# A fourth weight sum and the gate row's multiply-adds, moved behind the last addition to c

## The chip, the cores and the metric

The kernel runs on one core of one Trainium2 chip. Its time is device microseconds from start to end of one execution. The core has TensorE (PE in the profile), VectorE (DVE), ScalarE (ACT), GpSimd (POOL) and SyncE (SP), which here issues the transfers.

## What is computed

One layer: a modulated norm, attention of two kinds, an output projection with a gated residual, and then a gated feed-forward part. The change lies in the last, with 1024 tokens, 1024 channels and 2816 hidden channels:

```python
mod = jnp.dot(jax.nn.silu(c), w_ada[l]) + b_ada[l]
sh_a, sc_a, g_a, sh_m, sc_m, g_m = jnp.split(mod, N_MOD, axis=-1)
...
h = modulate(rmsnorm(x, g_mlp_norm[l]), sh_m, sc_m)
u = causal_dwconv(jnp.dot(h, w_up[l]), conv_w[l], conv_b[l])
gate, val = jnp.split(u, 2, axis=-1)
x = x + g_m[:, None, :] * jnp.dot(jax.nn.silu(gate) * val, w_down[l])
```

All of it is float32. The convolution is causal and has width 3. The vector g_m is the "gate row" of the change's name; it is needed only at the very end.

## The kernel before

The up projection runs over 22 tiles j of 128 gate channels and the 128 value channels that belong to them. Each tile is a 2 by 2 block product in the Strassen-Winograd form: seven products in place of eight, with sums of the weight blocks ahead of them and sums of the products behind them. So that full precision comes out of TensorE's fast float32 form, each operand is split into a high and a low half (`split`), and a product is three matmuls for each of four contraction blocks (`product`, L1067 to L1069), so 84 matmuls a tile.

`ff_tile(j, cur)` does the products of tile j, and between them prepares the weights of tile j+1:

- `ff_load` (L1072) loads two raw weight tiles and splits wa and wb. The high half is a copy on ScalarE (L77), the low half a subtraction on GpSimd (L84).
- `ff_sums` (L1081) makes the sums of the raw blocks on VectorE: L1084 gives wc, L1086 and L1087 give we and wd, and L1091 gives the fourth, wg, from a12 and the block that L1087 left. Each is split as above.
- VectorE adds the products up in `c`, a tile of four blocks: L1277, L1278, L1280 and last L1291, each with one operand in a PSUM bank. ScalarE copies two of the products (L1272 and L1287).
- `conv` (L1217), once for the gate channels and once for the value channels: ScalarE scales c into u (L1220), and VectorE adds the two shifted terms (L1221, L1222). Then come SiLU on ScalarE (L1295) and the product of the two halves on VectorE (L1296).
- The sums that the down projection will need are made on GpSimd: L1303 in even tiles, L1308, L1309 and L1311 in odd ones. They and the products go to DRAM through SyncE's queue (L1262).

`gate_row` is a generator. After two tiles each step loads two pieces of w_ada for the next step (L1196), and does two multiply-adds on VectorE over the two pieces loaded before (L1206 the first time, then L1208, into `gmbc`). Eight such steps are followed by an empty one, and by one that adds the bias (L448), sums over the partitions with TensorE (L449) and copies the row back (L1215). The main loop advances it by one step behind each tile from j = 2 on.

The order on each engine isn't that of the source: a scheduler places the instructions by their dependencies and by its own estimates of time, and the source can only add an order with `tc.issue_after(ins)`, which puts the block's instructions behind `ins` on `ins`'s engine alone. Before the change the scheduler put both L1091 and the gate row's multiply-adds ahead of L1291.

Of the kernel before, what the change touches and what calls it, by code (L numbers as in the profile page):

```python
# [22 lines left out]
MUL, ADD, SUB, MIN, MAX = ALU.mult, ALU.add, ALU.subtract, ALU.min, ALU.max  # L23
# [7 lines left out]
NF = FF // P  # L31
# [33 lines left out]
def layer_kernel(ctx, tc, I, out):  # L65
    nc = tc.nc
    pe, act, dve, pool, sp = nc.tensor, nc.scalar, nc.vector, nc.gpsimd, nc.sync
# [7 lines left out]
    def hi_of(eng, o, i):  # L75
        if eng == "a":
            act.activation(o, i, AF.Copy)  # L77
        elif eng == "p":
            pool.tensor_scalar(o, i, 1.0, 0.0, op0=MUL, op1=ADD)
        else:  # L80
            dve.tensor_copy(o, i)

    def lo_of(eng, o, i, hi):
        (pool if eng == "p" else dve).tensor_tensor(o, i, f32(hi), op=SUB)  # L84
# [30 lines left out]
    def rsqrt_mean(r, ss, n, cols=None):  # L115
        sc = ss if cols is None else ss[:, cols]
        pool.tensor_scalar(sc, sc, 1.0 / n, EPS, op0=MUL, op1=ADD)
        pool.tensor_tensor(r, ss, nhalf[:].to_broadcast(list(r.shape)), op=ALU.pow)
# [31 lines left out]
    def gemm3(pt, pairs, start=True, stop=True):  # L150

        n = len(pairs)
        for i, (sh, sl, mh, ml) in enumerate(pairs):
            pe.matmul(pt, sh, mh, start=(start and i == 0), stop=False)  # L154
            pe.matmul(pt, sh, ml, start=False, stop=False)  # L155
            last = pe.matmul(pt, sl, mh, start=False, stop=(stop and i == n - 1))  # L156
        anchor["pe"] = last.ins
# [119 lines left out]
    for d in range(ND):  # L277
# [22 lines left out]
        for t in range(NT):  # L300
            h, j = divmod(t, 4)
# [705 lines left out]
    def o_load(t):  # L1007
        ol[t] = go.tile([P, 4, P], F32R, name=f"ol{t}", tag="ol", bufs=4)
        oh[t] = go.tile([P, 4, P], F32R, name=f"oh{t}", tag="oh", bufs=4)
        anchor["ol"] = sp.dma_start(f32(ol[t][:]), oT_d[0:4, :, t * P:(t + 1) * P].rearrange("k p t -> p k t")).ins  # L1010
        hi_of("a", oh[t][:], f32(ol[t][:]))
        lo_of("p", ol[t][:], f32(ol[t][:]), oh[t][:])
# [29 lines left out]
    def bpage(nm, k, v, le):  # L1042
        pg = hpools[(nm, k)] if (nm, k) in hpools else h2p.tile([P, 2, 512], F32R, name=f"{nm}_{k}")
        hi_of("a", pg[:, 0], v[:])
        lo_of(le, pg[:, 1], v[:], pg[:, 0])
        B[nm, k] = pg
# [5 lines left out]
    def mt(tag, shape, name, dt=F32):  # L1052
        return mp["a" if tag in ("raw", "w2", "ws") else "b"].tile(list(shape), dt, name=name, tag=tag, bufs=MB[tag])
# [3 lines left out]
    def split(src, nm, tag="ws"):  # L1057
        w = mt(tag, [P, 2, 512], nm, F32R)
        hi_of("a", w[:, 0], src)
        lo_of("p", w[:, 1], src, w[:, 0])  # L1060
        return w
# [10 lines left out]
    def ff_load(j):  # L1072

        raw = []
        for i in range(2):
            r = mt("raw", [P, D], f"wu{i}_{j}")
            sp.dma_start(r[:], I["w_up"][i * NF + j].rearrange("p k m -> p (k m)"))
            raw.append(r)
        return raw, split(raw[0][:, :512], f"wa{j}", "w2"), split(raw[0][:, 512:], f"wb{j}", "w2")

    def ff_sums(j, raw):  # L1081
        a11, a12, a21, a22 = raw[0][:, :512], raw[0][:, 512:], raw[1][:, :512], raw[1][:, 512:]
        t3 = mt("s", [P, 512], f"ws3_{j}") if j else tb.tile([P, 512], F32, name="ws3_0", tag="v", bufs=12)
        dve.tensor_tensor(t3[:], a11, a21, op=SUB)  # L1084
        w = [split(t3[:], f"wc{j}")]
        dve.tensor_tensor(a21, a21, a22, op=ADD)  # L1086
        dve.tensor_tensor(a11, a21, a11, op=SUB)  # L1087
        w.append(split(a11, f"wd_{j}"))
        w.append(split(a21, f"we{j}"))
        w.append(split(a22, f"wf{j}"))  # L1090
        dve.tensor_tensor(a12, a12, a11, op=SUB)  # L1091
        w.append(split(a12, f"wg{j}"))
        return w

    op_ = {t: gb.tile([P, D], F32, name=f"pa{t}", tag="pa", bufs=4) for t in range(4)}

    def x_load(t):
        if t > 3:
            op_[t] = gb.tile([P, D], F32, name=f"pa{t}", tag="pa", bufs=4)
        sp.dma_start(op_[t][:], part_d[t])  # L1100
        ox[t] = tb.tile([P, D], F32, name=f"x1_{t}", tag="x1", bufs=8)
        sp.dma_start(ox[t][:], I["x"][t * P:(t + 1) * P, :])
# [4 lines left out]
    raw0, wa0, wb0 = ff_load(0)  # L1107
# [3 lines left out]
    w0 = None  # L1111
    for t in range(NT):
        pt = ps2.tile([P, 1024], F32, name=f"op{t}", tag="op", bufs=3)
        for n in range(2):
            gemm3(pt[:, n * 512:(n + 1) * 512],
                  [(oh[t][:, k], ol[t][:, k], wo[n][k][:, 0], wo[n][k][:, 1]) for k in range(4)])
        if t + 4 < NT:
            o_load(t + 4)
        pa, x1 = op_[t], ox[t]
        dve.tensor_tensor(pa[:], pa[:], pt[:], op=ADD)  # L1120
        dve.tensor_tensor(pa[:], pa[:], gabc[:], op=MUL)
        dve.tensor_tensor(x1[:], x1[:], pa[:], op=ADD)
        sp.dma_start(x1_d[t], x1[:])
        act.activation(pa[:], x1[:], AF.Square, accum_out=ss2[:, t:t + 1])
        if t + 4 < NT:
            x_load(t + 4)
        rsqrt_mean(r2[:, t:t + 1], ss2[:, t:t + 1], D)
        xn2[t] = x1
        dve.tensor_scalar(x1[:], x1[:], r2[:, t:t + 1], 1.0, op0=MUL, op1=MUL)
        if t == 1:  # L1130
            w0 = ff_sums(0, raw0)
        if t == 4:
            for k in range(ND):
                v0[k] = mod_T(k, 0)
                bpage("b11" if k < 4 else "b21", k % 4, v0[k], "v" if k % 2 else "p")
# [13 lines left out]
    p34 = ps2.tile([P, 1024], F32, name="p34_0", tag="op", bufs=3)  # L1149
# [37 lines left out]
    def bank(tag, name, n=1):  # L1187
        return ps3.tile([P, n * 512], F32, name=name, tag=tag, bufs=2 if tag == "p1" else 1)
# [75 lines left out]
    def ff_tile(j, cur):  # L1264
        wc, wd, we, wf, wg, wb, p1, c = cur
        p34 = bank("p34", f"p34_{j}", 2)
        p5, p6, p7 = bank("p5", f"p5_{j}"), bank("p6", f"p6_{j}"), bank("p7", f"p7_{j}")
        nxt = None
        if j:
            with tc.issue_after(p3_last[0]):  # L1270
                product(p1[:], wb, "b21", add=True)
            act.activation(c[:, 0], p1[:], AF.Copy)  # L1272
            if j == NF - 1:
                early()
            product(p7[:], wc, "t3")
            product(p6[:], wd, "t2")
            dve.tensor_tensor(c[:, 1], c[:, 3], p6[:], op=ADD)  # L1277
            dve.tensor_tensor(c[:, 2], c[:, 1], p7[:], op=ADD)  # L1278
            product(p5[:], we, "t1")
            dve.tensor_tensor(c[:, 1::2], c[:, 1:3], p5[:].unsqueeze(1).to_broadcast([P, 2, 512]), op=ADD)  # L1280
            product(p34[:, 512:], wf, "t4")
        if j + 1 < NF:
            raw, wa, wb = ff_load(j + 1)
            q1 = bank("p1", f"p1_{j + 1}")
            product(q1[:], wa, "b11")
            d = mt("c", [P, 4, 512], f"c{j + 1}")
            act.activation(d[:, 3], q1[:], AF.Copy)  # L1287
            nxt = ff_sums(j + 1, raw) + [wb, q1, d]
        if j:
            p3_last[0] = product(p34[:, :512], wg, "b22")  # L1290
            dve.tensor_tensor(c[:, 1:3], c[:, 1:3], p34[:].rearrange("p (a b) -> p a b", a=2), op=ADD)  # L1291
        cg = c[:, 0:2].rearrange("p a b -> p (a b)")
        cv = c[:, 2:4].rearrange("p a b -> p (a b)")
        ug, uv = conv(cg, j), conv(cv, NF + j)
        act.activation(ug[:], ug[:], AF.Silu)  # L1295
        dve.tensor_tensor(ug[:], ug[:], uv[:], op=MUL)  # L1296
        i = j // 2
        lo, hi = ug[:, :512], ug[:, 512:]
        sm = mt("s", [P, 512], f"gs{j}")
        if j % 2 == 0:  # L1300
            us.append(ug)
            keep(0, 1, i, lo)
            pool.tensor_tensor(sm[:], lo, hi, op=SUB)  # L1303
            keep(6, 1, i, sm[:])
        else:
            ue = us.pop()
            keep(1, 2, i, ug[:])
            pool.tensor_tensor(ue[:, 512:], ue[:, 512:], hi, op=ADD)  # L1308
            pool.tensor_tensor(ue[:, :512], ue[:, 512:], ue[:, :512], op=SUB)  # L1309
            keep(3, 2, i, ue[:])  # L1310
            pool.tensor_tensor(sm[:], lo, ue[:, :512], op=SUB)  # L1311
            keep(5, 1, i, sm[:])
        return nxt

    gr_gen = gate_row()
    p3_last = [last]
    cur = w0 + [None, None, c0]
    for j in range(NF):
        cur = ff_tile(j, cur)
        if j >= 2:  # L1320
            next(gr_gen, None)

    psC.__exit__(None, None, None)
    mlp.__exit__(None, None, None)
# [232 lines left out]
```

## Time and profile before

| what | value |
|---|---|
| runs shown | 1391.5, 1392.78, 1389.2 us (median 1391.5) |
| profiled execution | 1391.56 us, of which the span of instructions is 1389.8 us |
| TensorE, matmuls | 1233.6 us busy, 89% of the span |
| TensorE, weight loads | 1004.4 us, 72% |
| VectorE | 1112.7 us, 80% |
| ScalarE | 617.9 us, 44% |
| GpSimd | 694.8 us, 50% |
| up projection, tiles 2 to 21 | about 785 to 1180 us of the span |
| granted TensorE clock in that stretch | 1.00 |

Busy times are averages over stages of quite different kinds. For the up projection the order in time is read, tile by tile. A row of the timeline has the start in us, the duration in us, the engine, the line, the operation, the output and inputs by name, their shapes, how many such instructions are merged in the row, and in brackets the idle time of the engine ahead of it with what ended it. A row of the waits has the waiting instruction, what it waited for, the sum in us, how many times, and the longest. A row that begins with a line and ends with "x22" and three numbers has the shortest, middle and longest duration in ns.

### The profile page before, as it was taken

How to read it: one execution, taken by the hardware profiler on the slowest of the kernel's cores; microseconds unless marked ns; L12 is line 12 of the kernel's file. 1: busy time of each engine (PE TensorE's matmuls, PEld its weight loads, DVE VectorE, ACT ScalarE, POOL GpSimd, SP SyncE). 2: the span in 40 equal slices, each digit the busy share in tenths (PEclk: the TensorE clock that was granted, in tenths of full speed). 3: DMA queues.
4: the chain of work that ended last, by engine and by line, in shares of the span. 5: the costliest groups of instructions: out<-in, count | busy, mean ns of one | idle time of the engine just before them, and what ended most of it. 6: DMA issues, size and time to landing. Idle time of an engine off the chain costs nothing.

```text
span 1389.8 us, 18690 instructions
## 1 busy us (share of the span) xinstructions
PE 1233.6 (89%) x6156; PEld 1004.4 (72%) x6156; DVE 1112.7 (80%) x1870; ACT 617.9 (44%) x1129; POOL 694.8 (50%) x676
## 2 busy tenths in 40 slices
PE   4889798999777789886887999999999999999998
PEld 3888486987555577665665887777778777888886
DVE  6957888675689987794789798898888888688667
ACT  4343445443555544453365434434443444443331
POOL 5454557375546664353643666657867784200000
PEclk9899798999887889997999999999999999999999
DMA  8413658666313477678821233333223224984441
GB/s 314 131 37 85 142 143 188 155 146 138 74 41 78 87 158 164 127 146 237 302 100 53 91 129 99 121 129 114 99 99 107 84 99 139 322 326 129 129 159 61
DMA packets 223689, 190.57 MB, mean 137 GB/s; under 512 B 148708, under 2 KB 166884, under 8 KB 223592
## 3 DMA queue, kind: packets, MB, share of 16 engines
q1 hardware_dynamic: 223592, 189.38, 48.0%
q8 instruction: 48, 0.79, 0.2%
q14 instruction: 49, 0.40, 0.1%
HBM read 117.24 MB, written 37.49 MB: 111 GB/s over the span
## 4 chain that ended last, share of the span: by engine, by line
PE 40%; DVE 29%; issue 9%; DMA 7%; ACT 7%; POOL 6%; SPq 1%; DVEq 0%; POOLq 0%; ACTq 0%
DVE u L1222 4%; DVE u L1221 4%; PE dnA_P L1368 2%; PE dnA_P L1370 2%; PE dnA_P L1369 2%; PE p L1069 2%; PE p L1067 2%; PE p L1068 2%; PE sm L764 2%; PE sc L758 2%; PE dnB_P L1370 1%; PE dnB_P L1369 1%; PE dnB_P L1368 1%; ACT u L1220 1%; PE pvm L852 1%
## 5 line engine op out<-in xcount | busy, mean ns | idle before, releaser
L77 ACT ACTIVATE dnP<-dnr 128x1024 fp32r<-128x1024 f32 x73 | 77.3, 1061 | 110.9 <-PE dnA_P L1370 46.4
L1342 DVE TENSOR_TENSOR dnP<-dnr,dnP 128x1024 fp32r<-128x1024 f32 x72 | 88.2, 1229 | 46.9 <-ACT dnP L77 46.9
L1221 DVE SCALAR_TENSOR_TENSOR u<-c,cvp,u 128x1023 f32<-128x1023 f32 x44 | 81.7, 1897 | 43.9 <-ACT u L1220 43.9
L73 POOL TENSOR_SCALAR hlm<-Pm,rim 128x512 f16<-128x512 f32 (+3 forms) x96 | 68.4, 722 | 74.0 <-ACT Pm L790 21.0
L1222 DVE SCALAR_TENSOR_TENSOR u<-c,cvp,u 128x1022 f32<-128x1022 f32 x44 | 85.4, 1980 | 0.0
L73 POOL TENSOR_SCALAR hlc<-Pc,ric 128x640 f16<-128x640 f32 (+2 forms) x64 | 46.7, 733 | 69.0 <-DVE ric L793 45.2
L812 DVE SCALAR_TENSOR_TENSOR hlm<-Pm,rim,hlm 128x512 f16<-128x512 f32 (+3 forms) x96 | 67.5, 712 | 8.6 <-POOL hlm L73 8.2
L790 ACT ACTIVATE Pm<-sm,mm 128x128 f32<-128x128 f32 (+3 forms) x64 | 47.2, 738 | 52.1 <-DVE mm L783 26.7
L852 PE MATMUL pvm<-PTm,vt 128*128 128x256 f16 (+1 forms) x320 | 47.4, 301 | 20.9 <-DMA PTm<-hlm 16.8
L790 ACT ACTIVATE Pc<-sc,mc 128x640 f32<-128x640 f32 (+2 forms) x64 | 42.1, 659 | 49.7 <-DVE mc L779 36.5
L812 DVE SCALAR_TENSOR_TENSOR hlc<-Pc,ric,hlc 128x640 f16<-128x640 f32 (+2 forms) x64 | 53.6, 842 | 10.4 <-POOL hlc L73 10.2
L1220 ACT ACTIVATE u<-c,cvp 128x1024 f32<-128x1024 f32 x44 | 52.2, 1234 | 14.9 <-DVE c L1291 7.9
L852 PEld LDWEIGHTS <-vt 128*128 128x128 f16 x320 | 32.5, 111 | 36.2 <-issue 14.8
L77 ACT ACTIVATE wc<-ws 128x512 fp32r<-128x512 f32 x22 | 13.9, 633 | 98.4 <-DVE ws L1084 98.4
L154 PE MATMUL ipq<-wq_s,hT 128*128 128x256 f32 x192 | 55.5, 292 | 0.9 <-ACT wq_s L77 0.9
L155 PE MATMUL ipq<-wq_s,hT 128*128 128x256 f32 x192 | 55.8, 291 | 0.4 <-POOL wq_s L84 0.3
L156 PE MATMUL ipq<-wq_s,hT 128*128 128x256 f32 x192 | 55.3, 289 | 0.0
L1295 ACT ACTIVATE u<-u 128x1024 f32<-128x1024 f32 x22 | 23.4, 1062 | 67.8 <-DVE u L1222 67.8
L1369 PE MATMUL dnA_P<-dnP 128*128 128x512 f32 x132 | 51.3, 389 | 0.0
L1370 PE MATMUL dnA_P<-dnP 128*128 128x512 f32 x132 | 51.3, 389 | 0.0
L1368 PE MATMUL dnA_P<-dnP 128*128 128x512 f32 x132 | 51.2, 389 | 0.0
L84 POOL TENSOR_TENSOR wc<-ws,wc 128x512 fp32r<-128x512 f32 x22 | 35.4, 1611 | 30.5 <-ACT wc L77 30.5
(421 smaller groups left out, 4546.0 us busy)
## 6 DMA issues: line engine op xcount, KB each, us to landing
wu<-w_up SPq DMA_DIRECT2D x44, 512.0 KB, 3.5
dnr<-g_d SPq DMA_DIRECT2D x73, 256.0 KB, 3.6
aw<-w_ada SPq DMA_DIRECT2D x48, 256.0 KB, 3.8
g_d<-u SPq DMA_DIRECT2D x22, 512.0 KB, 2.8
dnr<-w_down SPq DMA_DIRECT2D x44, 256.0 KB, 5.4
adaw<-w_ada_a SPq DMA_DIRECT2D x16, 512.0 KB, 5.9
x<-x SPq DMA_DIRECT2D x16, 512.0 KB, 8.8
g_d<-gs SPq DMA_DIRECT2D x22, 256.0 KB, 2.2
```

Of the source, the lines that this page charges most:

```text
L73: pool.tensor_scalar(o, i, s, 1.0, op0=MUL, op1=MUL)
L77: act.activation(o, i, AF.Copy)
L790: act.activation(pr[:, :n], sv, AF.Exp, bias=m[:], scale=-1.0, accum_out=rsum[:, 0:1])
L812: dve.scalar_tensor_tensor(hl[:, w:2 * w], pp, ri[:], hl[:, :w], op0=MUL, op1=SUB)
L852: last = pe.matmul(dst, u.vst(j), mov, start=(x == 0), stop=(x == len(todo) - 1), skip_group_check=True)
L1220: act.activation(u[:], c, AF.Identity, scale=cvp[:, cv + 2:cv + 3], bias=cvp[:, cv + 3:cv + 4])
L1221: dve.scalar_tensor_tensor(u[:, 1:], c[:, :S - 1], cvp[:, cv + 1:cv + 2], u[:, 1:], op0=MUL, op1=ADD)
L1222: dve.scalar_tensor_tensor(u[:, 2:], c[:, :S - 2], cvp[:, cv:cv + 1], u[:, 2:], op0=MUL, op1=ADD)
L1342: r = f(*a, **k)
L1368: pe.matmul(pt, sh, w[:, 0, 0], start=start, stop=False, skip_group_check=add)
L1369: pe.matmul(pt, sh, w[:, 1, 0], start=False, stop=False, skip_group_check=add)
L1370: pe.matmul(pt, sl, w[:, 0, 0], start=False, stop=stop, skip_group_check=add)
```

## The change

`ff_sums` no longer makes the fourth sum itself, but returns a function that does. `ff_tile` calls it after L1291 has been issued, in a block that puts VectorE's instructions behind L1291. The step of the gate row, which stood behind the tile in the main loop, moves into the same block. Both stand ahead of `conv` in the source now. Tile 0, whose products are made before the loop, has no L1291; its call is not ordered.

```diff
         w.append(split(a22, f"wf{j}"))
-        dve.tensor_tensor(a12, a12, a11, op=SUB)
-        w.append(split(a12, f"wg{j}"))
-        return w
+
+        def rest():
+            dve.tensor_tensor(a12, a12, a11, op=SUB)
+            return split(a12, f"wg{j}")
+        return w, rest
...
-            w0 = ff_sums(0, raw0)
+            w0, rest = ff_sums(0, raw0)
+            w0.append(rest())
...
-            nxt = ff_sums(j + 1, raw) + [wb, q1, d]
+            nxt, rest = ff_sums(j + 1, raw)
         if j:
             p3_last[0] = product(p34[:, :512], wg, "b22")
-            dve.tensor_tensor(c[:, 1:3], c[:, 1:3], p34[:].rearrange("p (a b) -> p a b", a=2), op=ADD)
+            full = dve.tensor_tensor(c[:, 1:3], c[:, 1:3], p34[:].rearrange("p (a b) -> p a b", a=2), op=ADD).ins
+            with tc.issue_after(full):
+                if j + 1 < NF:
+                    nxt.append(rest())
+                if j >= 2:
+                    next(gr_gen, None)
+        else:
+            nxt.append(rest())
+        if j + 1 < NF:
+            nxt += [wb, q1, d]
         cg = c[:, 0:2].rearrange("p a b -> p (a b)")
         cv = c[:, 2:4].rearrange("p a b -> p (a b)")
         ug, uv = conv(cg, j), conv(cv, NF + j)
...
         cur = ff_tile(j, cur)
-        if j >= 2:
-            next(gr_gen, None)
```

Lines of the kernel before are used throughout: L1091 becomes L1093 in the changed kernel, L1291 becomes L1294, L1208 becomes L1211, L1220 to L1222 become L1223 to L1225, L1277 becomes L1280, L1287 becomes L1290 and L1296 becomes L1308.

## The prediction

> **What bounds the kernel now.** I read the page's chain that ended last, then the waits of the up projection (785 to 1180 us), then that stretch in order of time, engine by engine.
>
> ```profile
> PE 40%; DVE 29%; issue 9%; DMA 7%; ACT 7%; POOL 6%; SPq 1%; DVEq 0%; POOLq 0%; ACTq 0%
> ```
>
> ```profile
> DVE u L1221 <- ACT u L1220: 42.2, 20, 2.7
> DVE c L1291 <- PE p L1069: 2.7, 3, 1.7
> ```
>
> VectorE has one hole in a tile: 20 times, 2.1 us each, L1221 waits for ScalarE's L1220. The change puts VectorE work into just this hole. What the hole is used for today decides, and that stands in the order of time of tiles 5 and 6 (start, duration, engine, line):
>
> ```profile
> 851.21 1.40 DVE L1208 SCALAR_TENSOR_TENSOR gmbc<-adaw,cs,gmbc 128x512 f32<-128x512 f32 x2
> 852.53 0.68 DVE L1087 TENSOR_TENSOR wu<-wu,wu 128x512 f32<-128x512 f32 x1
> 853.32 0.69 DVE L1091 TENSOR_TENSOR wu<-wu 128x512 f32<-128x512 f32 x1
> 853.92 1.21 DVE L1291 TENSOR_TENSOR c<-c,p 128x1024 f32<-128x1024 f32 x1
> 857.67 3.52 DVE L1221 SCALAR_TENSOR_TENSOR u<-c,cvp,u 128x1023 f32<-128x1023 f32 x2 [2.53 <-ACT u L1220]
> 861.11 4.54 DVE L1222 SCALAR_TENSOR_TENSOR u<-c,cvp,u 128x1022 f32<-128x1022 f32 x2
> 865.75 1.23 DVE L1296 TENSOR_TENSOR u<-u,u 128x1024 f32<-128x1024 f32 x1
> 866.90 0.68 DVE L1277 TENSOR_TENSOR c<-c,p 128x512 f32<-128x512 f32 x1
> ...
> 870.37 1.67 DVE L1086 TENSOR_TENSOR wu<-wu 128x512 f32<-128x512 f32 x1
> ...
> 874.65 3.41 DVE L1208 SCALAR_TENSOR_TENSOR gmbc<-adaw,cs,gmbc 128x512 f32<-128x512 f32 x2
> 877.99 1.21 DVE L1291 TENSOR_TENSOR c<-c,p 128x1024 f32<-128x1024 f32 x1
> 880.57 4.55 DVE L1221 SCALAR_TENSOR_TENSOR u<-c,cvp,u 128x1023 f32<-128x1023 f32 x2 [1.37 <-ACT u L1220]
> 885.04 2.46 DVE L1222 SCALAR_TENSOR_TENSOR u<-c,cvp,u 128x1022 f32<-128x1022 f32 x2
> 887.61 1.22 DVE L1296 TENSOR_TENSOR u<-u,u 128x1024 f32<-128x1024 f32 x1
> ```
>
> ```profile
> 854.01 1.28 POOL L84 TENSOR_TENSOR wd<-wu,wd 128x512 fp32r<-128x512 f32 x1 [3.28 <-ACT wd L77]
> 855.24 1.30 POOL L84 TENSOR_TENSOR we<-wu,we 128x512 fp32r<-128x512 f32 x1
> 856.49 1.32 POOL L84 TENSOR_TENSOR wf<-wu,wf 128x512 fp32r<-128x512 f32 x1
> 857.74 2.36 POOL L84 TENSOR_TENSOR wa<-wu,wa 128x512 fp32r<-128x512 f32 x1
> 860.07 2.27 POOL L84 TENSOR_TENSOR wg<-wu,wg 128x512 fp32r<-128x512 f32 x1
> 862.30 2.27 POOL L84 TENSOR_TENSOR wb<-wu,wb 128x512 fp32r<-128x512 f32 x1
> 867.12 1.29 POOL L1308 TENSOR_TENSOR u<-u,u 128x512 f32<-128x512 f32 x1 [2.56 <-DVE u L1296]
> ```
>
> The same two L1222 take 2.46 us at 885 us, with GpSimd idle, and 4.54 us at 861 us, with GpSimd subtracting; GpSimd's subtractions take 2.3 us there instead of 1.3. The two engines take turns: one subtraction and one multiply-add come out every 2.24 us or so (857.74, 860.07, 862.30), 1.12 us each. L1208 at 874.65 pays the same price: 3.41 us for the two instead of 1.40, so 1.70 a turn, 1.12 of it GpSimd's and 0.58 its own. L1291 does not collide, since it reads a PSUM bank:
>
> ```profile
> L1291 DVE TENSOR_TENSOR c<-c,p x21: 1206/1214/1222, 774.9 to 1175.3; 128x1024 f32<-128x1024 f32 x21
> ```
>
> So the hole isn't empty. While VectorE does L1291 and then waits, GpSimd runs wd, we and wf 1.24 us apart, at full speed. What is queued is not VectorE but VectorE and GpSimd together. The fourth weight sum, on the other hand, has the cheapest place there is now: GpSimd is waiting for ScalarE's wd, which needs L1087, and so L1091 runs alone (minimum, median and maximum in ns):
>
> ```profile
> L1091 DVE TENSOR_TENSOR wu<-wu x22: 691/692/1758, 667.5 to 1156.8; 128x512 f32<-128x512 f32 x22
> ```
>
> **The Trainium skill** gives the reason on its page "SBUF — State Buffer", section "Who interferes with whom": a Vector instruction with two SBUF inputs contends with a GpSimd instruction that reads SBUF, and the one that starts first holds the pair for its whole instruction. The trace agrees that they exclude each other, but has 2.24 us for a turn of both where the durations alone, 1.28 and 1.20, would add to 2.48. An estimate by that rule, with whole durations as holds, stands at the end of the next part.
>
> **The change part by part.** The built program's order shows that it does what it says: on VectorE L1091 and the gate row's two multiply-adds stand right behind L1291, ahead of both L1221; on ScalarE the high half of wg moves behind both L1220; GpSimd's order is unchanged. Two things come along: in seven gate tiles L1277 moves ahead of L1296, and in some of them TensorE's twelve matmuls of wb come ahead of the last two of wc.
>
> *The fourth sum, a tile without gate row.* I walk from the end of L1087 (853.21) to the end of L1296 (866.98): 13.77 us now. GpSimd's wd begins 0.80 later, L1221 at 4.46 with wd, we and wf behind it. From there turns of 1.12: L1221 to 5.58, wa 6.70, L1221 7.82, wg 8.94, L1222 10.06, wb 11.18, L1222 12.30, then L1296, 1.33 with its gap: 13.63, 0.14 short of the trace. Afterwards: L1291 from 0 to 1.13, wd holds until 1.97, L1091 until 2.53 (a 0.56 turn), we 3.65. Now wf has been asked for before L1220 is done: ScalarE drops wg from its queue ahead of L1220,
>
> ```profile
> 855.88 0.62 ACT L77 ACTIVATE wg<-wu 128x512 fp32r<-128x512 f32 x1
> 856.40 2.37 ACT L1220 ACTIVATE u<-c,cvp 128x1024 f32<-128x1024 f32 x2
> ```
>
> which brings the first L1220 0.52 us forward (856.40 to 855.88), so L1221 is ready at 3.94, but wf has the turn until 4.77. L1221 then ends at 5.89, and six turns and L1296 later it is 13.94. That is 0.17 over the trace, 0.31 over the walk of before; I take 0.24. The 0.7 us that L1091 frees ahead of L1291 is used by nobody, since GpSimd waits for wd through it. In every second tile TensorE's product for L1291 is about due anyway, and L1291 cannot use it fully either; the walk does not change, as wd sets the next turn. Ten such tiles, 2.4 us; with everything absorbed 0, with the 0.7 us lost as well as 0.3, some 7.
>
> *The gate row.* Both walks start at the end of L1086 and take in L1277. Odd tile: now 866.98 - 851.21 + 0.61 = 16.4. After: L1087 0.72, L1291 1.85, wd 2.62, L1091 3.18, we 4.30, L1208 4.88, wf 6.00, L1208 6.58, wa 7.70, four multiply-adds and wg, wb in turns to 14.4, L1277 15.1, L1296 16.4. Nothing gained: the multiply-adds that ran alone at 851.21 now each wait for a subtraction. Even tile, from 872.04 to 888.83 and 0.61: 17.4 now, 17.35 after. There they collide already (3.41 us), so moving them is even.
>
> *L1277 ahead of L1296.* GpSimd waits for L1296 (its 2.56 us at 867.12) and then works through L1277, L1278 and L1280, all PSUM reads, without collision. With L1277 in front, 0.6 us of that cover is gone and L1084 meets a subtraction: walked, 0.3 us in one tile of a pair and 0.4 in the other. Four pairs: 2.6 us; bounds 0 and 5.
>
> *One more gate tile that costs.* The first gate pair now lies in a tile that TensorE bounds:
>
> ```profile
> 793.89 1.22 DVE L1291 TENSOR_TENSOR c<-c,p 128x1024 f32<-128x1024 f32 x1 [1.66 <-PE p L1069]
> ...
> 809.88 0.87 DVE L1206 TENSOR_SCALAR gmbc<-adaw,cs 128x512 f32<-128x512 f32 x2
> ...
> 812.93 1.22 DVE L1291 TENSOR_TENSOR c<-c,p 128x1024 f32<-128x1024 f32 x1 [0.78 <-PE p L1069]
> ...
> 1175.31 1.22 DVE L1291 TENSOR_TENSOR c<-c,p 128x1024 f32<-128x1024 f32 x1
> ```
>
> L1291 still waits 0.78 us behind L1206, so it is free. Behind the L1291 at 812.93 it delays a convolution that nothing covers: 1.4 us (two ops at the 851.21 row's price), bounds 0 and 3.4 (the 874.65 row).
>
> *The rest at nothing.* The closing ops of the gate row
>
> ```profile
> L448 DVE TENSOR_TENSOR gmbc<-gmbc,brow 1x512 f32<-1x512 f32 x2 | 2.3, 1140 | 0.0
> ```
>
> move behind L1291 too and pay there what they pay now, give or take 1 us. The gate row's loads stand one tile earlier in SyncE's queue, still behind the store of u; their buffers, seven to four a tile, were freed a tile before. wg's low half, and with it the load that reuses its raw buffer, ends up to 1.2 us later; its readers come a tile later.
>
> Sum: 2.4 + 2.6 + 1.4 = 6.4 us. The profiled execution took 1391.56 us, the median is 1391.5: 1398.0 us.
>
> By the skill's whole-instruction lock the fourth sum would cost 0.80 + 1.28 + 0.69 + 1.28 + 1.28 - 4.46 = 0.87 a tile, an estimate, and the time would be about 1404 us; no row shows holds that long.
>
> **The rivals.** *The hole is filled for nothing (faster).* If VectorE were what bounds, 18 tiles would save 0.69 each (12.4), and eight gate tiles 1.32 where the hole is 2.53 and 0.68 where it is 1.37 (8.0). TensorE stops that: 793.89 to 812.93, 19.04 us, is a tile in which L1291 waits for it, and 18 of these are 342.7 of the 362.4 us from 812.93 to 1175.31, so at most 19.7 us, about 1372. For it speaks the wait list; against it that GpSimd uses the hole. It decides if a subtraction beside L1091 or L1208 costs under half a turn. Chance 0.12, most of it partial, 1380 to 1387.
>
> *An even exchange.* The turns are the same in number, only their order changes; then 1391.6, and the trace's rows for L1091 grow by what the hole shrinks. Chance 0.22.
>
> *TensorE loses as well (slower still).* With wb ahead of wc's end TensorE stalls on ScalarE's L1287 with more left to do; if L1291 then waits for it in every second tile, some 0.7 us in nine tiles, 6 us more: 1404. Chance 0.10; my forecast has 0.56.
>
> **How the numbers follow.** A measurement of this kernel tells some 0.3%, 4.2 us, from no change: below 1387.3 is faster, above 1395.7 slower. Slower holds the forecast and the last rival, 0.66; same 0.22; faster 0.12. The range, 1389 to 1404, leaves out the faster case and the upper bounds taken together.
>
> **What would show it.** Right: the wait of L1221 for L1220 falls from 42.2 us to well under half, L1091's median rises from 692 ns to 1.2 us or more, L1208's lone 0.74 us ones vanish, wd, we and wf lose their 1.3 us, and L1291 starts in non-gate tiles lie over 39.5 us apart by twos. Wrong: L1091 stays near 0.7 us behind L1291, or the L1291 starts close to 19.04 us.

## The result and the profile after

The changed kernel took 1402.8 us in the middle of its first six runs, against 1390.35 us for the kernel before: ratio 1.0081 (95% interval 1.0052 to 1.0109), slower. Twelve more runs on another occasion, beside new runs of the kernel before, gave 1.0050 (1.0034 to 1.0066), some 7 us. The forecast was 1398.0 us, 6.4 us up.

The profiled execution of the changed kernel took 1406.06 us with a span of 1404.3 us. Most of what follows measures one stretch, from the first start of the last addition to c (L1291 before, L1294 changed) to its last, 20 tiles on. Its ends stand at the right of the row of that line, in us:

```profile
L1294 DVE TENSOR_TENSOR c<-c,p x21: 1207/1214/1222, 781.1 to 1189.8; 128x1024 f32<-128x1024 f32 x21
```

408.7 us. In the kernel before the timeline has the first of these starts at 774.85 and the last at 1175.31 (both rounded in its row in the prediction): 400.5 us. So the stretch lost 8.3 us (408.72 against 400.46). Behind it the two profiles agree: 214.5 us from the last of these additions to the end in both. Ahead of it the changed kernel's profile is 6.2 us later; that part is taken up under the last experiment.

VectorE's waits in the up projection (785 to 1195 us) show that the hole was filled:

```profile
DVE u L1224 <- ACT u L1223: 11.4, 10, 1.4
DVE c L1294 <- PE p L1069: 8.7, 7, 4.1
```

The wait ahead of the convolution fell from 42.2 us to 11.4, yet the stretch became longer. Where the time went is in the durations of the moved instructions (shortest, middle and longest in ns):

```profile
L1093 DVE TENSOR_TENSOR wu<-wu x22: 682/1572/1597, 671.3 to 1172.0; 128x512 f32<-128x512 f32 x22
```

```profile
L1211 DVE SCALAR_TENSOR_TENSOR gmbc<-adaw,cs,gmbc x14: 1775/1784/1790, 842.0 to 973.7; 128x512 f32<-128x512 f32 x14
```

The fourth sum went from 692 ns to 1572, and no multiply-add of the gate row runs alone any more: their middle went from 744 ns to 1784. In the order of time, tile 5 (the first L1294 here is the one at 853.92 us before), VectorE and then GpSimd:

```profile
858.03 1.59 DVE L1086 TENSOR_TENSOR wu<-wu 128x512 f32<-128x512 f32 x1
859.73 0.69 DVE L1087 TENSOR_TENSOR wu<-wu,wu 128x512 f32<-128x512 f32 x1
860.34 1.21 DVE L1294 TENSOR_TENSOR c<-c,p 128x1024 f32<-128x1024 f32 x1
861.47 1.57 DVE L1093 TENSOR_TENSOR wu<-wu 128x512 f32<-128x512 f32 x1
862.96 3.50 DVE L1211 SCALAR_TENSOR_TENSOR gmbc<-adaw,cs,gmbc 128x512 f32<-128x512 f32 x2
866.38 4.54 DVE L1224 SCALAR_TENSOR_TENSOR u<-c,cvp,u 128x1023 f32<-128x1023 f32 x2
870.85 3.50 DVE L1225 SCALAR_TENSOR_TENSOR u<-c,cvp,u 128x1022 f32<-128x1022 f32 x2
874.28 0.67 DVE L1280 TENSOR_TENSOR c<-c,p 128x512 f32<-128x512 f32 x1
874.87 1.21 DVE L1308 TENSOR_TENSOR u<-u,u 128x1024 f32<-128x1024 f32 x1
```

```profile
861.22 1.27 POOL L84 TENSOR_TENSOR wd<-wu,wd 128x512 fp32r<-128x512 f32 x1 [2.15 <-ACT wd L77]
862.45 1.74 POOL L84 TENSOR_TENSOR we<-wu,we 128x512 fp32r<-128x512 f32 x1
864.16 1.75 POOL L84 TENSOR_TENSOR wf<-wu,wf 128x512 fp32r<-128x512 f32 x1
865.87 1.74 POOL L84 TENSOR_TENSOR wa<-wu,wa 128x512 fp32r<-128x512 f32 x1
```

VectorE has no hole at all from 859.73 us to the end of L1308 at 876.08. The subtractions we, wf and wa, which started 1.25 us apart while VectorE waited (we and wf took 1.3 us each), now start 1.71 us apart, each one taking turns with the sum or a multiply-add. Nothing starts earlier: the first L1224 starts 6.8 us behind the end of L1086 (866.38 less 859.62), and before the change the first L1221 started 6.5 us behind it (857.67 less 851.21, where the instruction behind L1086 starts), with the same VectorE instructions in between.

### The profile page after: what moved, and what is told of

The parts are those of the page before. It is cut to its first block, busy times and chain, and to the rows that moved or that the text cites. A ratio compares the mean times of both kernels' runs of the same rounds, so it can differ in the third digit from the quotient of the medians.

```text
span 1404.3 us, 18703 instructions
## 1 busy us (share of the span) xinstructions
PE 1238.7 (88%) x6156; PEld 1008.9 (72%) x6156; DVE 1146.1 (82%) x1870; ACT 617.7 (44%) x1129; POOL 713.3 (51%) x676
## 4 chain that ended last, share of the span: by engine, by line
PE 45%; DVE 31%; issue 8%; DMA 7%; ACT 4%; POOL 4%; SPq 1%; DVEq 0%; ACTq 0%; POOLq 0%
DVE u L1224 4%; PE p L1067 3%; PE p L1069 3%; PE p L1068 3%; DVE u L1225 3%; PE dnA_P L1378 2%; PE dnA_P L1379 2%; PE dnA_P L1380 2%; PE sc L758 2%; PE sm L764 2%; DVE gmbc L1211 2%; PE pvc L852 2%; DMA PTm<-hlm 2%; PE dnB_P L1379 1%; PE dnB_P L1378 1%
## 5 line engine op out<-in xcount | busy, mean ns | idle before, releaser
L1224 DVE SCALAR_TENSOR_TENSOR u<-c,cvp,u 128x1023 f32<-128x1023 f32 x44 | 91.5, 2118 | 12.4 <-ACT u L1223 12.4
L1225 DVE SCALAR_TENSOR_TENSOR u<-c,cvp,u 128x1022 f32<-128x1022 f32 x44 | 83.3, 1932 | 0.0
L1223 ACT ACTIVATE u<-c,cvp 128x1024 f32<-128x1024 f32 x44 | 52.1, 1234 | 11.6 <-DVE c L1294 9.4
L84 POOL TENSOR_TENSOR wa<-wu,wa 128x512 fp32r<-128x512 f32 x22 | 41.6, 1890 | 19.0 <-ACT wa L77 19.0
```

The source lines that it names most:

```text
L1224: dve.scalar_tensor_tensor(u[:, 1:], c[:, :S - 1], cvp[:, cv + 1:cv + 2], u[:, 1:], op0=MUL, op1=ADD)
L1225: dve.scalar_tensor_tensor(u[:, 2:], c[:, :S - 2], cvp[:, cv:cv + 1], u[:, 2:], op0=MUL, op1=ADD)
```

## The experiments

All are measured by the same row, first and last start of the addition to c. The one program that was profiled twice, the changed kernel, repeats it to 0.1 us. Differences are taken from the starts in the timeline, to a hundredth. e3 to e7 were executed once each: there the stretch is the evidence, not the whole time.

**The sum alone** (e1). The gate row's step goes back behind the tile:

```diff
             with tc.issue_after(full):
                 if j + 1 < NF:
                     nxt.append(rest())
-                if j >= 2:
-                    next(gr_gen, None)
...
         cur = ff_tile(j, cur)
+        if j >= 2:
+            next(gr_gen, None)
```

> Only the fourth weight sum moves behind L1291; the gate row's multiply-adds stay where the scheduler put them in the kernel before, and L1277 stays behind L1296. Measured from the first L1291 to the last one (400.5 us before, 408.7 us changed). Theory 1 (VectorE's instructions with two SBUF inputs and GpSimd's subtractions take turns; in the old place the sum runs alone, in the new one it costs GpSimd or VectorE a turn): some 0.3 to 0.4 us a tile in 18 tiles, 405.5 to 407.5 us, and the middle duration of the sum at 1.1 to 1.6 us. Theory 2 (the gate row and the later L1308-type product carry the loss, the sum is free in the hole): 400 to 401 us. Rival from the prediction (the hole is filled for nothing): under 395 us.

```profile
L1294 DVE TENSOR_TENSOR c<-c,p x21: 1202/1208/1221, 780.8 to 1187.7; 128x1024 f32<-128x1024 f32 x21
```

```profile
L1093 DVE TENSOR_TENSOR wu<-wu x22: 677/1372/1725, 672.9 to 1170.0; 128x512 f32<-128x512 f32 x22
```

406.9 us, 6.5 over the kernel before and inside the range of theory 1, and the ratio of the times is 1.0049 (1.0026 to 1.0072). VectorE's wait for ScalarE fell to 20.1 us all the same. So the sum is not free in the hole.

**The gate row alone** (e2). The sum stays where it was:

```diff
-            dve.tensor_tensor(c[:, 1:3], c[:, 1:3], p34[:]..., op=ADD)
+            full = dve.tensor_tensor(c[:, 1:3], c[:, 1:3], p34[:]..., op=ADD).ins
+            with tc.issue_after(full):
+                if j >= 2:
+                    next(gr_gen, None)
...
         cur = ff_tile(j, cur)
-        if j >= 2:
-            next(gr_gen, None)
```

> Only the gate row's two multiply-adds move behind L1291; the fourth sum stays ahead of it, and L1277 stays behind L1296. First to last L1291. Theory 1, walked with turns of 1.12 us: an odd gate tile gains 0.55 us and an even one 0.7, since the multiply-adds fill the wait for L1220 while the sum keeps its cheap place; four pairs gain 4 to 5 us, and the gate pair that now falls behind the L1291 of tile 3 costs 1.4: 396 to 398.5 us, 2 to 4 us under the kernel before. Theory 2 (the gate row carries the loss): 404 to 406 us.

```profile
L1291 DVE TENSOR_TENSOR c<-c,p x21: 1210/1214/1224, 770.1 to 1165.4; 128x1024 f32<-128x1024 f32 x21
```

395.3 us, 5.2 under the kernel before, a little below the expected range; the ratio is 0.9963 (0.9942 to 0.9984). This half of the change is a gain. The two middle pairs of gate tiles gain 1.2 us each. The order of time in one of them, VectorE and GpSimd, shows how:

```profile
846.32 0.69 DVE L1091 TENSOR_TENSOR wu<-wu 128x512 f32<-128x512 f32 x1
846.93 1.21 DVE L1291 TENSOR_TENSOR c<-c,p 128x1024 f32<-128x1024 f32 x1
848.06 2.51 DVE L1208 SCALAR_TENSOR_TENSOR gmbc<-adaw,cs,gmbc 128x512 f32<-128x512 f32 x2
850.67 4.37 DVE L1221 SCALAR_TENSOR_TENSOR u<-c,cvp,u 128x1023 f32<-128x1023 f32 x2
```

```profile
847.02 1.30 POOL L84 TENSOR_TENSOR wd<-wu,wd 128x512 fp32r<-128x512 f32 x1 [1.38 <-ACT wd L77]
848.27 1.75 POOL L84 TENSOR_TENSOR we<-wu,we 128x512 fp32r<-128x512 f32 x1
849.98 1.75 POOL L84 TENSOR_TENSOR wf<-wu,wf 128x512 fp32r<-128x512 f32 x1
```

The sum still runs alone (0.69 us), while GpSimd waits for wd's high half. L1291 covers wd. So when the multiply-adds come, one subtraction is already done, the first slips in, and L1221 starts as soon as the last is through. The rest of the gain comes of the gate row standing one tile later: the first pair gains 2.3 us and the last loses 0.6, and the tiles behind the gate row gain 1.0.

**The collision taken out of both kernels** (e3 and e4). The low halves of the weight splits in the up projection are left out, zeros stand in their place:

```diff
     def split(src, nm, tag="ws"):
         w = mt(tag, [P, 2, 512], nm, F32R)
         hi_of("a", w[:, 0], src)
-        lo_of("p", w[:, 1], src, w[:, 0])
+        pool.memset(f32(w[:, 1]), 0.0)
```

> The kernel before, but GpSimd's low halves of the weight splits in the up projection are not computed: GpSimd fills them with zero instead, an instruction of the same size that reads no SBUF. Theory 1 (the two engines exclude each other over what they read): the multiply-adds L1221 and L1222 run at 1.1 to 1.3 us each, and the tiles fall to TensorE's 19.04 us: first to last L1291 381 to 385 us. If it were GpSimd's or VectorE's own busy time that bounds, or ScalarE's order, 395 to 401 us.

> The changed kernel with the same replacement as the run before this one (zeros in place of the low halves of the weight splits). Theory 1: within 1 us of that run, 381 to 385 us, as the loss of 8.2 us is one of turns alone. Rival (the loss comes of ScalarE's later wg, of L1277 ahead of L1296, or of TensorE's order with wb ahead of the end of wc): 3 to 8 us above that run.

First the kernel before, then the changed one, each with the fill:

```profile
L1291 DVE TENSOR_TENSOR c<-c,p x21: 1220/1221/1222, 765.3 to 1145.2; 128x1024 f32<-128x1024 f32 x21
```

```profile
L1294 DVE TENSOR_TENSOR c<-c,p x21: 1220/1220/1222, 763.3 to 1143.1; 128x1024 f32<-128x1024 f32 x21
```

379.8 us both, a little under the 381 to 385 expected: the difference of 8.3 us between the two orders is gone, and so are 20.6 us of the kernel before. In the group rows of VectorE with the fill in the kernel before, L1222's mean is 1278 ns (it was 2050), and what VectorE waits for now is TensorE. The second view is the changed kernel with the fill:

```profile
L1222 DVE SCALAR_TENSOR_TENSOR u<-c,cvp,u 128x1022 f32<-128x1022 f32 x38 | 47.0, 1278 | 0.0
...
L1291 DVE TENSOR_TENSOR c<-c,p 128x1024 f32<-128x1024 f32 x19 | 23.2, 1221 | 61.9 <-PE p L1069 61.9
```

```profile
L1294 DVE TENSOR_TENSOR c<-c,p 128x1024 f32<-128x1024 f32 x19 | 23.2, 1221 | 81.9 <-PE p L1069 81.9
```

What ScalarE does later, what TensorE does in another order, and L1277 ahead of L1296 are all still in the second of these kernels, and cost nothing there. That doesn't make them free elsewhere: with 61.9 and 81.9 us of waiting for TensorE, a loss of 0.4 us a tile would be covered whatever its cause, and the next run finds that L1277's place does cost. Nor do these two runs separate reading nothing from having less to do: a fill took 0.53 us and a subtraction 1.24. That the engines exclude each other rests on the rows of turns, not on this pair.

**The order that came along** (e5). L1277 is held behind the product of the two halves:

```diff
-            dve.tensor_tensor(c[:, 1], c[:, 3], p6[:], op=ADD)
+            with tc.issue_after(mul_last[0]):
+                dve.tensor_tensor(c[:, 1], c[:, 3], p6[:], op=ADD)
...
-        dve.tensor_tensor(ug[:], ug[:], uv[:], op=MUL)
+        mul_last[0] = dve.tensor_tensor(ug[:], ug[:], uv[:], op=MUL).ins
```

> The changed kernel, with the one order that came along taken back: L1277 is held behind the tile's last product L1296 in every tile. First to last L1291 (400.5 us before, 408.7 changed, 406.9 with the sum alone moved, 395.3 with the gate row alone moved). If L1277 ahead of L1296 costs the 1.2 us a pair that the two traces show between the end of L1296 and the end of L1086 (5.03 and 4.50 us against 4.45 and 3.9 with L1277 taken off), seven tiles give back some 4 us: 404 to 405.5 us. If the scheduler put it there at no cost: 408 to 409 us. If it is the whole of what the sum and the gate row do to one another (408.7 against 400.5 + 6.5 - 5.2 = 401.8): about 402 us.

```profile
L1295 DVE TENSOR_TENSOR c<-c,p x21: 1206/1209/1222, 777.5 to 1182.3; 128x1024 f32<-128x1024 f32 x21
```

404.8 us, 3.9 less. Two things stand behind that number. In the gate tiles the hold gives back 4.6 us. In the last tile it costs 0.7 (19.65 us against 18.92): there L1277 stood ahead of L1296 before the change too (1169.20 us against 1172.07), and the hold moves it from there as well. So 4.6 of the 8.3 us were L1277's, and the other 3.7 are what sum and gate row cost together. These don't add up from the parts: alone they come to +6.5 and -5.2, so 1.3. Behind the gate row's gain the sum costs 8.8 us (404.1, without the last tile's 0.7, against 395.3), 2.3 more than alone. The rows above fit that it takes the first place behind L1291, in which a multiply-add slips in at e2; no run swaps the two, so this is not shown.

**wb's low half on VectorE, and more** (e6, e7, e8). If turns are what is scarce, fewer should help more than any order. A low half is 0.6 us of VectorE alone and a turn of 1.12 us of GpSimd:

```diff
-    def split(src, nm, tag="ws"):
+    def split(src, nm, tag="ws", le="p"):
         w = mt(tag, [P, 2, 512], nm, F32R)
         hi_of("a", w[:, 0], src)
-        lo_of("p", w[:, 1], src, w[:, 0])
+        lo_of(le, w[:, 1], src, w[:, 0])
...
-    ... split(raw[0][:, 512:], f"wb{j}", "w2")
+    ... split(raw[0][:, 512:], f"wb{j}", "w2", "v")
```

> The kernel before, with wb's low half subtracted on VectorE instead of GpSimd (same arithmetic). Theory 1 (turns): VectorE pays some 0.6 us and is spared a GpSimd turn of 1.12 us, so 0.5 us a tile in 18 tiles, 390 to 393 us from the first to the last L1291 (400.5 before). Rival (VectorE's own work bounds the tile): 0.6 us a tile more, about 411 us.

> The gate row alone behind L1291, and wb's low half on VectorE. Theory 1: both gains add until TensorE's 19.04 us a tile stops them: 384 to 388 us from the first to the last L1291. Rival (the wait for L1220 was the only thing to gain): 395 us or more.

> As the run before this one, with wa's low half on VectorE too. Theory 1: most tiles at TensorE's 19.04 us, 380 to 384 us from the first to the last L1291, so 16 to 20 us under the kernel before. Rival (VectorE bounds now, with a hole again behind ScalarE's L1220): 390 us or more.

e6 has this edit alone, e7 adds e2's, e8 adds wa in the same way. In this order:

```profile
L1291 DVE TENSOR_TENSOR c<-c,p x21: 1207/1217/1222, 769.3 to 1160.0; 128x1024 f32<-128x1024 f32 x21
```

```profile
L1291 DVE TENSOR_TENSOR c<-c,p x21: 1212/1221/1222, 778.1 to 1163.1; 128x1024 f32<-128x1024 f32 x21
```

```profile
L1291 DVE TENSOR_TENSOR c<-c,p x21: 1205/1207/1222, 766.0 to 1148.0; 128x1024 f32<-128x1024 f32 x21
```

390.7, 385.0 and 382.0 us. VectorE got more to do each time, and the stretch shorter, by 9.8, 15.4 and 18.4 us, each inside its expected range. So VectorE's own work was not the bound. 20 tiles at TensorE's 19.04 us are 380.8, so the last is about at its end. e8 took 1368.4 us against 1391.5: ratio 0.9851 (0.9816 to 0.9886), the fastest version that computes everything, and faster than both kernels of this case. Most of its collisions are gone, as VectorE's group row shows, with a mean of 1274 ns:

```profile
L1222 DVE SCALAR_TENSOR_TENSOR u<-c,cvp,u 128x1022 f32<-128x1022 f32 x38 | 46.9, 1274 | 0.0
```

**The changed kernel again** (e9), for the 6.2 us ahead of the stretch.

> The changed kernel once more, for the part of its loss that lies outside the stretch between the first and the last L1291. The first executions gave 12.5 us between the medians, their profiles 8.3 us between first and last L1291 and 6.2 us ahead of it, where the two programs are the same. If those 6.2 us are scatter from run to run, the stretch stays at 408.7 us within 0.3, the first L1291 lies anywhere between 763 and 781 us as in the other profiles, and the median is 7 to 10 us above the kernel before. If the change costs time ahead of the stretch too, the first L1291 is at 779 us or later again, and the median 11 us or more above.

```profile
L1294 DVE TENSOR_TENSOR c<-c,p x21: 1207/1214/1222, 768.2 to 1177.0; 128x1024 f32<-128x1024 f32 x21
```

The stretch is 408.8 us again, and its start 768.2 us, 12.8 earlier than in the first profile of the same program. The median was 1400.4 us against 1393.5, 6.9 us up and so at the lower end of what was expected. The time ahead of the stretch scatters from run to run: the six profiles that leave the weight splits as they are begin the stretch between 768.2 and 781.1 us. Part of it is TensorE's clock (rows: window, then busy time and count of PE, PEld, DVE, ACT, POOL, then the granted clock). Around the first matmuls with wb, in the first profile of the changed kernel and in this one:

```profile
764.00:771.00 7.00, 5.24 (x16) 4.17 (x17) 5.61 (x4) 2.85 (x5) 4.70 (x3) 0.76 0.27 97
```

```profile
753.00:760.00 7.00, 5.48 (x24) 4.53 (x25) 5.84 (x4) 2.62 (x4) 4.73 (x3) 1.00 0.25 90
```

With a clock of 0.76 these matmuls came 0.43 us apart instead of 0.23, and the tile lost 1.6 us against the kernel before. As the same program had 1.00 there the second time, that is chance, not the change. What scatters further ahead, in the attention, was not followed up.

## Why the prediction was right

By its own steps:

- *What is queued is VectorE and GpSimd together.* Shown by the rows of turns and by e6: giving VectorE work of GpSimd's makes the tile shorter. That taking GpSimd's subtractions out takes the difference out (e3, e4) fits it. The wait of 42.2 us that the change aimed into tells nothing by itself: e1 and e2 both bring it down by half (20.1 and 23.9 us), and one loses and the other gains.
- *The fourth sum, 0.24 us a tile, 2.4 us in tiles without gate row.* From the end of L1087 to the end of L1296 the walk said 13.94 us, and the changed profile has 14.17 (1131.03 to 1145.20 us) against 13.77: 0.40 a tile, so the step was too small by 0.16. The difference lies in GpSimd's row: from the start of wd to the start of wa it takes 4.21 us (1131.83 to 1136.04), where the walk had 3.97 and the kernel before 3.74. The sum's turn stands between wd and we. The ten tiles at the end of the stretch lost 2.35 us nevertheless. The closing of the gate row, put at nothing, gained 0.6 in two tiles (40.28 us against 40.84), and the two behind them ran even (39.43 against 39.50); how is told in the last section. At 0.40 in each of the ten the term would have been 4, so that it came out at 2.35 is luck.
- *The gate row, nothing gained.* The two walks said 16.4 us for an odd tile and 17.35 for an even one; the changed profile has 16.46 and 17.34. But it isn't the gate row that makes them so. By itself it gains 5.2 us (e2). The walk was right for the two together, and laid the blame unevenly: the prediction counted the sum only where there is no gate row.
- *L1277 ahead of L1296, 2.6 us.* Mis-sized: 4.6 us (e5, in the gate tiles). From the end of L1296 to the end of L1086 the profile has 5.03 and 4.50 us, against 4.45 and 3.9 before with L1277 taken off. All of L1277's 0.6 us is lost in each tile, not half of it.
- *One more gate tile, 1.4 us.* About right: with L1277 taken back (e5), the two middle gate pairs run even with the kernel before (42.09 us against 42.06, 42.12 against 42.04). The first gains 0.7 (40.25 against 40.99) and the last loses 1.9 (42.13 against 40.23). So the gate row standing one tile later costs 1.2 us.
- *The sum, 6.4 us.* The eight gate tiles lost 5.9 us instead of 4.0, the others 2.35 instead of 2.4, so 8.3 together. The forecast is about half of the 12.5 us between the first medians, and close to the 7 us of the second set. That the other 4 us of the first set are scatter from ahead of the stretch fits e9, but isn't shown run by run.

The rival that ends faster had its condition: a subtraction beside L1091 or L1208 should cost under half a turn. It cost most of one: 0.88 us for L1091 (1572 ns against 692) and 1.04 for L1208 (1784 against 744), where a turn is 1.12. The rival in which TensorE loses as well came in part: behind the gate tiles, L1294 waits 0.4 us for TensorE in every second tile, not 0.7 in nine; the longest part of the 8.7 us is one wait of 4.1 us, which the last section tells of. By the page "SBUF — State Buffer" of the Trainium skill, section "Who interferes with whom", with whole durations as holds, the sum's move would have cost 0.87 us a tile, by the prediction's estimate. The rows have 0.40, so the exclusion holds in these tiles, at a price nearer to that of the turns (0.24).

The signs named ahead came with one exception: the wait fell to 11.4 us, L1091's middle rose to 1572 ns, no L1208 runs alone, and the last tiles without gate row lie 39.9 us apart by twos. Only wd kept its 1.3 us, since it starts ahead of the sum (861.22 and 861.47 us).

## What to carry to other kernels

A wait in one engine's queue is a free place for work only if no other engine depends on it: look at what the engine beside it does at full speed during that wait. Here the cheapest place for the fourth sum, a VectorE instruction with two SBUF inputs, was not VectorE's wait but GpSimd's, and the best was to make fewer such turns. When a change has two halves, run each alone: this one held a gain of 5 us and a loss of 6.5.

## What was not expected of the hardware

Turns are not always taken. In the tile that closes the gate row, VectorE and GpSimd of the changed kernel:

```profile
1012.42 1.59 DVE L1093 TENSOR_TENSOR wu<-wu 128x512 f32<-128x512 f32 x1
1013.93 2.38 DVE L448 TENSOR_TENSOR gmbc<-gmbc,brow 1x512 f32<-1x512 f32 x2
1016.24 2.46 DVE L1224 SCALAR_TENSOR_TENSOR u<-c,cvp,u 128x1023 f32<-128x1023 f32 x2
1018.63 2.46 DVE L1225 SCALAR_TENSOR_TENSOR u<-c,cvp,u 128x1022 f32<-128x1022 f32 x2
```

```profile
1013.42 1.74 POOL L84 TENSOR_TENSOR we<-wu,we 128x512 fp32r<-128x512 f32 x1
1015.12 7.12 POOL L84 TENSOR_TENSOR wf<-wu,wf 128x512 fp32r<-128x512 f32 x1
1022.20 2.27 POOL L84 TENSOR_TENSOR wa<-wu,wa 128x512 fp32r<-128x512 f32 x1
```

GpSimd's wf takes 7.12 us, while the four multiply-adds of L1224 and L1225 go through at their lone 1.2 us. VectorE then came early to the next L1294 and waited 4.1 us for TensorE. The same 7.1 us stand in e5 and e9, and in no tile of the other kernels' up projections. The two L448, over one partition, stand ahead of it in all three, but they don't explain it alone: e2 has them behind L1291 as well, and its we and wf took 1.75 and 1.74 us there. And in e5 a subtraction for tile 0, ahead of the stretch, lost its turn beside VectorE instructions over all partitions (GpSimd, then the first and one of the last of VectorE's row beside it):

```profile
727.65 17.46 POOL L84 TENSOR_TENSOR wa<-wu,wa 128x512 fp32r<-128x512 f32 x1 [8.66 <-ACT wa L77]
```

```profile
727.62 0.69 DVE L84 TENSOR_TENSOR t<-hv,t 128x512 fp32r<-128x512 f32 x1
...
742.66 0.70 DVE L1170 TENSOR_TENSOR hv<-hv,hv 128x512 f32<-128x512 f32 x1
```

VectorE's instructions there came 0.60 us apart without a break up to 743.26 us, and the subtraction ended at 745.11. In the kernel before, the same subtraction took 1.80 us, and the VectorE instruction that met it 1.77. What decides whether the turn is given stays open.

And the stretch of 20 tiles repeats within 0.1 us in the two profiles of the changed kernel (408.7 and 408.8), while the 770 us ahead of it differ by 12.8. For a change of half a per cent, the stage in the profile told more than the medians of six runs.
